# A decoder trunk in one core: the order of each stage's last sums, and where weights and memory are placed between stages

## The chip, the cores and the metric

The kernel runs on one core of a Trainium2 chip. The metric is the time of one execution in microseconds on the device; a time without further words is the median of several executions.

## The reference

Two layers work on 512 tokens of 1024 features, with 256 memory tokens beside them. Each layer is four steps, and each step ends in a layer normalization with a gain and a bias; `a` is the square root of 2.

```python
for i in range(DEPTH):                      # DEPTH = 2
    x = layer_norm(a * x + 0.5 * swiglu_ffn(x, ffn_w_in[i, 0], ffn_w_out[i, 0]), ...)
    h = diff_attention(x, ...) if i == 0 else pool_mixer(x, ...)
    x = layer_norm(a * x + h, ...)
    x = layer_norm(a * x + memory_cross_attention(x, mem, xa_wq[i], xa_wkv[i], xa_wo[i]), ...)
    x = layer_norm(a * x + 0.5 * swiglu_ffn(x, ffn_w_in[i, 1], ffn_w_out[i, 1]), ...)
```

`swiglu_ffn` is `(silu(x @ Wg) * (x @ Wu)) @ w_out` with 2816 hidden features. `diff_attention` (DA) has 8 heads with a rotary embedding and subtracts a second softmax from the first. `pool_mixer` takes causal means over 2, 4, 8 and 16 tokens and a small matrix for each group. `memory_cross_attention` has 4 heads, whose keys and values come from the memory. All is float32.

## The kernel before

**Numbers.** Every factor of a product is split in two parts of 32 bits with a shorter mantissa: `wh` or `xh`, a cast on ScalarE (L107), and `wl` or `xl`, the rest, a subtraction on VectorE (L108). A product is three matmuls (L163, L164, L165: high by high, low by high, high by low).

**Tiling.** The stream lies in four tiles `X` of 128 tokens by 1024 features. Weights come through DMA queues of SyncE (SP) and, where two blocks are added on the way, GpSimd (POOL), into raw tiles (`ra`, `rc`, `b`, `raw`), and are split into `wh` and `wl`. The FFN's matrices are multiplied by seven products of blocks in place of eight; lanes x, y and z are its products in work, and its factors of the stream (`factors`: `xh`, `xl`, `xe`) are sums and differences of blocks of X, made in `turn_factors` (L471 to L482). For that, X is transposed by TensorE (`pt<-ident,X`, L366), 128 by 128 at a time, eight for a token. `wh` of cross attention's keys and queries is made by L203 and L205.

**Stages.** There are eight: FFN, DA, cross attention, FFN; FFN, pool mixer, cross attention, FFN. Each stage ends with its *last sums*: for each token tile t and each half of the features, a matmul tile `ps` (18 matmuls of 512 columns in an FFN, 12 in attention) that VectorE adds to X (L312). After both halves of a token comes its LayerNorm, in `ln_token`: a mean (VectorE, L321), a Square with its sum (ScalarE, L328), two small GpSimd operations for the reciprocal root (L329, L330), and two scalings on VectorE, each in two instructions of 512 columns (L333, L336). Gain and bias are loaded in halves of 512 columns. For DA and cross attention as the next stage, the token is then transposed and split in `turn`. FFNs transpose and split all four tokens themselves at their start, with four ScalarE copies (L422) that keep raw blocks. In FFNs the sums are ordered by half and then by token; in the mixers' and attention's last half by token and then by half.

**Order.** Each engine has a queue, and works through it in order. The order in the queues is planned ahead by a scheduler, from the program's order, priorities and pools: a tile in a pool that takes over other tiles' place waits for their last readers. Cross attention's output weights (`raw<-in_xa_wo`, 4 x 512 rows) are split into tiles of the pool `w`, which FFN weights take over after it. `weave` runs a main sequence (keys and values of the memory, in layer 1) with a side sequence (pool mixer) between.

Of the kernel before, what the change touches and what calls it, by code (L numbers as in the profile page):

```python
# [44 lines left out]
GATES = {"xa": (1, 2)}  # L45

# [51 lines left out]
class Trunk:  # L98
# [33 lines left out]
    @contextmanager  # L132
    def stage_pools(self, raw, aux, w=5):

        pool = lambda name, **k: self.tc.tile_pool(name=name, bufs=1, reuse_waits="tile", **k)
        with pool("w") as self.wp, pool("raw") as self.rawp, pool("aux", space=PSUM) as self.auxp:
            self.w_bufs, self.raw_bufs, self.aux_bufs, self.aux_turn = w, raw, aux, 0
            yield
# [20 lines left out]
    def mm3(self, out, w, x, start, stop, again=False):  # L159
# [5 lines left out]
        mm(out, w[1], x[0], start=False, stop=stop, skip_group_check=again)  # L165
# [81 lines left out]
    def rows(self, w, k0, kn, c0):  # L247

        got = []
        for k in range(0, kn, 4):  # L250
# [29 lines left out]
    def load_row(self, tag, row):  # L280

        if tag in ("hr", "sr"):
            t = self.tmp(tag, (P, 2, S))
            got = [t[:, half] for half in range(2)]
        else:
            got = [self.tmp(tag) for _ in range(2)]
        for half, t in enumerate(got):
            src = row[None, half * S : (half + 1) * S]
            self.nc.sync.dma_start(t, src.to_broadcast([P, S]))
        return got  # L290

    def begin_ln(self, layer, i, scale):

        self.ln_scale = scale
# [10 lines left out]
        self.make_xt = not self.last_ln and self.ln_next in ("da", "xa")  # L305
# [10 lines left out]
    def ln_token(self, t):  # L316
# [5 lines left out]
        y = [X[:, half * S : (half + 1) * S] for half in range(2)]  # L322
# [8 lines left out]
        for half in range(2):  # L331
            c = slice(half * S, (half + 1) * S)
            nc.vector.scalar_tensor_tensor(y[half], X[:, c], mean, g[half], ALU.add, ALU.mult)  # L333
        for half in range(2):
            c = slice(half * S, (half + 1) * S)
            end = nc.vector.scalar_tensor_tensor(X[:, c], y[half], rstd, b[half], ALU.mult, ALU.add)  # L336
# [5 lines left out]
        if self.make_xt:  # L342
            self.late.append(t)

# [7 lines left out]
    def new_xt(self):  # L352
        self.xh = [self.xtp.tile([P, 4, S], F32R, tag="xh", name="xh") for _ in range(2)]
        self.xl = [self.xtp.tile([P, 4, S], F32R, tag="xl", name="xl") for _ in range(2)]

    def turn(self, t, half, two_pass=None):

        pt = self.aux("pt").rearrange("p (c n) -> p c n", c=4)
        c0 = half * S
        self.transpose4(pt, [self.X[t][:, c0 + j * P : c0 + (j + 1) * P] for j in range(4)])  # L360
        o = slice(t * P, (t + 1) * P)
        self.turned = self.split(self.xh[half][:, :, o], self.xl[half][:, :, o], pt)
# [6 lines left out]
    def to_tokens(self, parts, w, k0, kn, first, last, scale):  # L369

        nc = self.nc
        order = [(half, t) for half in range(2) for t in range(NT)]
        ws = [None, None]
        if last and kn == 4:
            order.sort(key=lambda x: x[1])
        for half, t in order:
            c, o = slice(half * S, (half + 1) * S), slice(t * P, (t + 1) * P)
            if t == 0:
                ws[half] = self.rows(w, k0, kn, half * S)
# [4 lines left out]
            if last:  # L384
                self.ln_add(t, half, scale if first else 1.0, ps)
                if half == 1:
                    if t < NT - 1:
                        self.turn_late()
                    self.ln_token(t)
# [7 lines left out]
    def ffn(self, layer, j, ln, beside=None):  # L397
        w_in, w_out = self.a["ffn_w_in"][layer, j], self.a["ffn_w_out"][layer, j]
        self.new_xt()
# [16 lines left out]
        for w in works + works[:1]:  # L416
            next(w)
        raw = [self.tmp("hb", (P, 4, 2 * P)) for _ in range(2)]
        pts = [self.turn_factors(t) for t in range(2)]
        for t in range(2):  # L420
            for half in range(2):
                self.nc.scalar.copy(raw[half][:, :, t * P : (t + 1) * P], pts[t][half])  # L422
# [20 lines left out]

    def factor_tiles(self):


        parts = []
        for x in (self.xh, self.xl):
            views = [t.rearrange("p a (b n) -> p (a b) n", n=2 * P) for t in x]
            got = [v[:, i : i + 4] for v in views for i in (0, 4)]  # L450
            parts.append(got + [self.act("xe", (P, 4, 2 * P)) for _ in range(3)])
        return list(zip(*parts))

    def turn_factors(self, t, raw=None):
# [5 lines left out]
        for half in range(2):  # L460
            tag = "px" if t in (0, 3) else ("py", "yz")[half]
            pt = self.aux("pt", tag).rearrange("p (c n) -> p c n", c=4)
            self.transpose4(pt, [self.X[t][:, half * S + j * P : half * S + (j + 1) * P] for j in range(4)])
            pts.append(pt)
        if t < 2:
            for half, pt in enumerate(pts):
                self.split(F[half][0][:, :, o], F[half][1][:, :, o], pt)
            return pts
# [16 lines left out]
    def up(self, w, u, lane, early):  # L485
# [19 lines left out]
        def operand(raw):  # L505
            v = self.hl([P, 4, H])
            self.split(v[0], v[1], raw)
# [13 lines left out]
        bank = lambda t: t.rearrange("p (j n) -> p j n", j=2)  # L521

# [6 lines left out]
        v = operand(ra)  # L529
        more(ra, 1, 2)  # L530
# [153 lines left out]
    def plain_down(self, w, layer, j, ln):  # L684
# [11 lines left out]
        for half in range(2):  # L696
# [14 lines left out]
            for t in range(NT):  # L711
                o = slice(t * P, (t + 1) * P)
# [624 lines left out]
```

## Time and profile before

| | us |
|---|---|
| median of 3 executions | 2026.42 (2024.79 to 2027.14) |
| the profiled execution | 2023.37 |
| its span, first to last instruction | 2021.6 |

| engine | busy share of the span |
|---|---|
| TensorE (PE), matmuls | 97% |
| TensorE, weight loads | 89% |
| VectorE (DVE) | 78% |
| ScalarE (ACT) | 51% |
| GpSimd (POOL) | 16% |

How to read the lines below: times run from the span's start. A timeline row has start, duration, engine, line of the kernel, operation, output<-inputs (without buffer numbers), partitions x elements, count, and in brackets the idle time ahead and what ended it. A row of waits has who waited for whom and the total, the number and the longest. PE's starts, not its durations, give its rate, since matmuls overlap.

### The profile page before, as it was taken

What the parts mean: (1) busy time and instruction counts of PE and PEld (TensorE: products, weight loads), DVE (VectorE), ACT (ScalarE), POOL (GpSimd) and SP (SyncE); (2) the same over time, 40 slices, a digit from 0 to 9 for tenths busy, and PEclk for the clock granted to TensorE, in tenths of its full rate; (3) what the DMA queues carried; (4) which work ended last, traced back from release to release, by engine and by line L of the source; (5) the groups of instructions that cost most, each with busy time, mean ns of one, the idle gap of its engine ahead of it and who ended that gap; (6) DMA issues with size and microseconds to landing.
All of it is one profiled execution on the core that took longest, in us unless ns stands there. A gap on an engine that the chain in (4) does not pass through costs nothing.

```text
span 2021.6 us, 32634 instructions
## 1 busy us (share of the span) xinstructions
PE 1961.3 (97%) x13104; PEld 1799.4 (89%) x13104; DVE 1570.6 (78%) x2260; ACT 1027.6 (51%) x1561; POOL 315.1 (16%) x305
## 2 busy tenths in 40 slices
PE   8999999999999998999999999999999999999997
PEld 8999998887878987999998899999799878999996
DVE  8988887888866548788887788888786566888885
ACT  6545454566645426554553555545454335555452
POOL 2111110122110002121121211111100013111211
PEclk9999999999999998999999999999989998999999
DMA  9877763222115335977774677876333319677861
GB/s 277 169 167 167 169 134 107 64 63 84 53 53 167 105 122 128 189 167 167 157 157 129 136 163 167 168 170 133 127 114 126 104 64 204 151 162 162 186 128 42
DMA packets 248455, 277.96 MB, mean 137 GB/s; under 512 B 8432, under 2 KB 212720, under 8 KB 248304
## 3 DMA queue, kind: packets, MB, share of 16 engines
q0 software_dynamic: 92928, 92.29, 29.7%
q1 hardware_dynamic: 155376, 183.59, 28.0%
q8 instruction: 103, 1.69, 0.3%
q14 instruction: 48, 0.39, 0.1%
HBM read 273.75 MB, written 2.10 MB: 136 GB/s over the span
## 4 chain that ended last, share of the span: by engine, by line
PE 67%; issue 19%; DVE 7%; ACT 4%; POOL 2%; DMA 1%; SPq 0%; POOLq 0%; DVEq 0%; ACTq 0%
PE x L165 8%; PE x L164 8%; PE x L163 8%; PE z L165 4%; PE z L164 4%; PE z L163 4%; PE px L163 3%; PE px L164 3%; PE px L165 3%; PE y L165 2%; PE ps L163 2%; PE y L163 2%; PE y L164 2%; PE ps L164 2%; PE ps L165 2%
## 5 line engine op out<-in xcount | busy, mean ns | idle before, releaser
L107 ACT CAST wh<-ra 128x1024 fp32r<-128x1024 f32 x184 | 193.1, 1049 | 235.3 <-PE x L164 70.1
L503 POOL DMA_DIRECT2D ra<-in_ffn_w_in_dram x132 | 170.1, 1312 | 839.3 <-DVE wl L108 797.4
L108 DVE TENSOR_TENSOR wl<-ra,wh 128x1024 fp32r<-128x1024 f32 x184 | 223.3, 1220 | 79.0 <-ACT wh L107 79.0
L107 ACT CAST wh<-rc 128x1024 fp32r<-128x1024 f32 x136 | 142.4, 1050 | 140.8 <-PE x L164 43.9
L163 PE MATMUL x<-xh,wh 128*128 128x256 f32 x704 | 202.3, 288 | 5.7 <-ACT wh L107 4.6
L165 PE MATMUL x<-xh,wl 128*128 128x256 f32 x704 | 202.3, 287 | 1.5 <-DVE wl L108 1.4
L164 PE MATMUL x<-xl,wh 128*128 128x256 f32 x704 | 201.9, 287 | 0.3 <-DVE xl L108 0.3
L165 PE MATMUL x<-xe,wl 128*128 128x256 f32 x704 | 199.2, 283 | 0.0
L164 PE MATMUL x<-xe,wh 128*128 128x256 f32 x704 | 199.2, 283 | 0.0
L163 PE MATMUL x<-xe,wh 128*128 128x256 f32 x704 | 199.1, 283 | 0.0
L107 ACT CAST wh<-b 128x1024 fp32r<-128x1024 f32 x112 | 117.5, 1049 | 153.2 <-PE x L164 77.8
L108 DVE TENSOR_TENSOR wl<-rc,wh 128x1024 fp32r<-128x1024 f32 x136 | 164.7, 1219 | 36.5 <-ACT wh L107 36.5
L108 DVE TENSOR_TENSOR wl<-b,wh 128x1024 fp32r<-128x1024 f32 x112 | 136.9, 1223 | 50.9 <-ACT wh L107 50.4
L108 DVE TENSOR_TENSOR wl<-raw,wh 128x1024 fp32r<-128x1024 f32 x76 | 95.3, 1263 | 69.5 <-ACT wh L107 68.8
L163 PEld LDWEIGHTS x<-xh,wh 128*128 128x128 f32 x704 | 137.8, 196 | 7.9 <-ACT wh L107 5.2
L165 PEld LDWEIGHTS x<-xh,wl 128*128 128x128 f32 x704 | 137.6, 196 | 2.6 <-DVE wl L108 2.6
L164 PEld LDWEIGHTS x<-xl,wh 128*128 128x128 f32 x704 | 137.7, 196 | 1.8 <-DVE xl L108 0.7
L164 PEld LDWEIGHTS x<-xe,wh 128*128 128x128 f32 x704 | 135.0, 192 | 1.3
L163 PEld LDWEIGHTS x<-xe,wh 128*128 128x128 f32 x704 | 135.0, 192 | 1.2
L165 PEld LDWEIGHTS x<-xe,wl 128*128 128x128 f32 x704 | 135.0, 192 | 0.0
L107 ACT CAST wh<-raw 128x1024 fp32r<-128x1024 f32 x76 | 79.2, 1049 | 92.0 <-PE xq L164 26.5
L329 POOL TENSOR_SCALAR var<-var 128x1 f32<-128x1 f32 x32 | 20.0, 626 | 584.4 <-ACT p L328 298.0
(372 smaller groups left out, 6237.2 us busy)
## 6 DMA issues: line engine op xcount, KB each, us to landing
ra<-in_ffn_w_in_dram POOLq DMA_DIRECT2D x132, 512.0 KB, 7.0
rc<-in_ffn_w_in_dram SPq DMA_DIRECT2D x88, 512.0 KB, 5.4
b<-in_ffn_w_out_dram SPq DMA_DIRECT2D x76, 512.0 KB, 4.4
ra<-in_ffn_w_in_dram SPq DMA_DIRECT2D x44, 512.0 KB, 3.7
rc<-in_ffn_w_in_dram POOLq DMA_DIRECT2D x44, 512.0 KB, 9.4
raw<-in_xa_wkv_dram SPq DMA_DIRECT2D x16, 1024.0 KB, 5.4
raw<-in_da_w_qkv_dram SPq DMA_DIRECT2D x16, 512.0 KB, 5.0
raw<-in_xa_wq_dram SPq DMA_DIRECT2D x8, 1024.0 KB, 4.8
```

Of the source, the lines that this page charges most:

```text
L107: self.nc.scalar.copy(hi, src),
L108: self.nc.vector.tensor_sub(lo, src, hi.bitcast(F32)),
L163: mm(out, w[0], x[0], start=start, stop=False, skip_group_check=again)
L164: mm(out, w[0], x[1], start=False, stop=False, skip_group_check=again)
L165: mm(out, w[1], x[0], start=False, stop=stop, skip_group_check=again)
L329: nc.gpsimd.tensor_scalar(var, var, 1.0 / D, EPS * self.ln_scale**2, ALU.mult, ALU.add)
L503: nc.gpsimd.dma_start(t, source(*block), accum_op=ALU.add)
```

## The change

1. The last sums of all stages come in one order, by (half, token): (0,0), (0,1), (1,0), (1,1), (0,2), (0,3), (1,2), (1,3). Token 0 is transposed just after the sum (0,3) was put in the queue and token 1 after (1,2).
2. FFNs take part in this: tokens 0 and 1 are transposed and split at the end of the stage before, and the FFN rebuilds their raw blocks by two additions xh + xl of 1024 columns on VectorE, in place of four ScalarE copies. These additions are placed behind the first weights' split.
3. Gain and bias are loaded as one tile of 1024 columns, and the scalings are one instruction each, save in the pool mixer and the last LayerNorm. Cross attention has a tag of its own for them (`gb`).
4. The last half of cross attention's output weights is split into tiles of the heads' tags (`q`, `kv`, `pT`), eight splits of 512 columns in place of four of 1024.
5. In layer 1 the order of the pools is raw, memory, weights; the memory is loaded first in the pool mixer at a high priority, and `weave` has other numbers (900 and 4300 for 1200).
6. Transposes and pool matmuls are placed behind the last matmul put out before them (`behind`); side pools wait by tile.

```diff
+LAST = ((0, 0), (0, 1), (1, 0), (1, 1), (0, 2), (0, 3), (1, 2), (1, 3))
+TURNS = ((0, 3), (1, 2))
...
-    def weave(self, main, side, gap):
+    def weave(self, main, side, gap, lead=0):
...
-        self.clock, credit, weight = 0, 0, 1.0
+        self.clock, credit, weight = 0, -lead, 1.0
...
+            if homes:
+                got += [home() for home in homes]
+                for j, t in enumerate(got):
+                    self.split(t[0], t[1], raw[:, j])
+                continue
...
-        self.make_xt = not self.last_ln and self.ln_next in ("da", "xa")
+        self.make_xt = not self.last_ln and self.ln_next != "pool"
...
+        if self.last_ln or not self.wide_gain:
+            cols = [slice(half * S, (half + 1) * S) for half in range(2)]
+        else:
+            cols = [slice(0, D)]
...
-        for half in range(2):
-            c = slice(half * S, (half + 1) * S)
-            nc.vector.scalar_tensor_tensor(y[half], X[:, c], mean, g[half], ALU.add, ALU.mult)
+        for i, c in enumerate(cols):
+            nc.vector.scalar_tensor_tensor(y[i], X[:, c], mean, g[i], ALU.add, ALU.mult)
...
+    def summed(self, half, t, scale, ps):
+
+        self.ln_add(t, half, scale, ps)
+        if self.late and (half, t) in TURNS:
+            self.turn_late(1 if (half, t) == TURNS[0] else 0)
+        if half:
+            self.ln_token(t)
...
+        with self.behind() if self.last_mm else nullcontext():
+            self.transpose4(pt, [self.X[t][:, c0 + j * P : c0 + (j + 1) * P] for j in range(4)])
...
-        order = [(half, t) for half in range(2) for t in range(NT)]
-        if last and kn == 4:
-            order.sort(key=lambda x: x[1])
-        for half, t in order:
+        for half, t in LAST if last else sorted(LAST):
...
+        self.turn_late(2)
+        self.late = []
+        next(works[0])
         raw = [self.tmp("hb", (P, 4, 2 * P)) for _ in range(2)]
-        pts = [self.turn_factors(t) for t in range(2)]
-        for t in range(2):
-            for half in range(2):
-                self.nc.scalar.copy(raw[half][:, :, t * P : (t + 1) * P], pts[t][half])
-        self.turn_factors(2, raw)
-        next(works[0])
-        self.turn_factors(3, raw)
+        act, dve = self.first_split
+        with self.tc.issue_after(act.ins), self.tc.issue_after(dve.ins):
+            for r, (hi, lo) in zip(raw, self.factors):
+                self.nc.vector.tensor_tensor(r, hi.bitcast(F32), lo.bitcast(F32), ALU.add)
+            self.turn_factors(2, raw)
         for w in works[1:]:
             next(w)
+        self.turn_factors(3, raw)
...
+        kv = lambda: tuple(self.kvp.tile([P, S], F32R, tag="kv", name="kv", bufs=8) for _ in range(2))
+        q, pT = (lambda: self.pair("q")), (lambda: self.pair("pT"))
+        homes = [[q] * 4, [kv, kv, kv, pT]]
...
-            self.later.enter_context(self.other_pools())
+            self.later.enter_context(self.other_pools(("raw", "mem", "w")))
...
                 side = self.pool_mixer(layer, ln)
+                with self.tc.high_priority():
+                    self.load_memory()
                 next(side)
-                self.load_memory()
                 self.kv = []
-                self.weave(self.early_kv(layer, 2), side, 1200)
+                self.weave(self.early_kv(layer, 2), side, 900, 4300)
```

More of the change, by code (lines that the diff above doesn't have):

```diff
@@ L384, in to_tokens @@
             if last:
[L385 to L389, printed above, removed]
+                self.summed(half, t, scale if first else 1.0, ps)
             else:
@@ L442, in ffn, with factor_views, turn_factors @@
         drain(works[0])
+    def factor_views(self):
+        views = [t.rearrange("p a (b n) -> p (a b) n", n=2 * P) for t in self.xh + self.xl]
+        got = [v[:, i : i + 4] for v in views for i in (0, 4)]
+        return list(zip(got[:4], got[4:]))
     def factor_tiles(self):
[L447 to L454, printed above, removed]
+        new = lambda: [self.act("xe", (P, 4, 2 * P)) for _ in range(3)]
+        return self.factor_views() + list(zip(new(), new()))
+    def turn_factors(self, t, raw):
         nc, F = self.nc, self.factors
@@ L506, in operand @@
             v = self.hl([P, 4, H])
-            self.split(v[0], v[1], raw)
+            splits.append(self.split(v[0], v[1], raw))
             return v
@@ L529, in up @@
         v = operand(ra)
+        if early and lane == 0:
+            self.first_split = splits[0]
         more(ra, 1, 2)
@@ L695, in plain_down, with operands @@
         self.begin_ln(layer, ln, 2.0)
-        for half in range(2):
+        def operands(half):
             ws = []
```

133 lines of the change are left out of this document (73 added, 60 removed).

## The prediction

> **What bounds the kernel now.** I read the page first, then the waits of TensorE stretch by stretch, the windows around the eight stage ends, and the timeline at four of them.
>
> ```profile
> span 2021.6 us, 32634 instructions
> PE 1961.3 (97%) x13104; PEld 1799.4 (89%) x13104; DVE 1570.6 (78%) x2260; ACT 1027.6 (51%) x1561; POOL 315.1 (16%) x305
> L107 ACT CAST wh<-ra 128x1024 fp32r<-128x1024 f32 x184 | 193.1, 1049 | 235.3 <-PE x L164 70.1
> out_dram<-X SPq DMA_DIRECT2D x8, 256.0 KB, 2.1
> ```
>
> TensorE is busy for 97% of the span and the change leaves its work alone, so only the holes can move, and they lie where one stage hands over to the next. The waits of TensorE there (total, times, longest), one fence for each hand-over: cross attention to second FFN in layer 0, first FFN to pool mixer, cross attention to second FFN in layer 1.
>
> ```profile
> PE pt L366 <- ACT hb L422: 4.6, 1, 4.6
> PE x L163 <- ACT wh L107: 2.3, 1, 2.3
> ```
> ```profile
> PE pp L1038 <- ACT xh L107: 2.8, 1, 2.8
> PE pp L1041 <- DVE xl L108: 2.7, 1, 2.7
> ...
> PE pt L1079 <- DVE X L312: 1.0, 1, 1.0
> ```
> ```profile
> PE z L163 <- DVE hr L545: 3.9, 1, 3.9
> ```
>
> Next, windows from the end of a stage's last sums (T0) to a milestone behind the hole: kernel start; first FFN to DA; DA to cross attention; into layer 0's second FFN; into layer 1's first FFN; pool mixer; into layer 1's second FFN. Columns: window, its length, busy time (count) by engine, granted clock, DMA share, GB/s.
>
> ```profile
> 0.00:42.20 42.20, 34.08 (x247) 32.68 (x248) 32.86 (x49) 29.06 (x42) 9.30 (x12) 0.96 1.06 292
> 340.00:360.00 20.00, 19.05 (x120) 16.04 (x119) 17.75 (x33) 8.38 (x15) 5.81 (x10) 1.00 0.19 60
> 604.80:622.10 17.30, 15.49 (x130) 14.79 (x128) 15.34 (x24) 10.76 (x16) 1.29 (x2) 1.00 0.56 182
> 771.40:811.70 40.30, 32.81 (x246) 31.36 (x244) 32.96 (x46) 28.82 (x42) 12.11 (x11) 0.87 0.74 171
> 1117.10:1153.70 36.60, 31.75 (x249) 30.64 (x248) 31.08 (x46) 24.89 (x40) 8.96 (x9) 0.95 0.49 119
> 1458.90:1480.00 21.10, 14.68 (x92) 13.63 (x90) 19.40 (x36) 12.69 (x21) 2.79 (x4) 0.76 0.59 185
> 1661.30:1703.80 42.50, 34.00 (x245) 32.70 (x243) 33.35 (x46) 28.31 (x42) 12.04 (x11) 0.88 0.97 229
> ```
>
> TensorE's rate, and the clock after a hole:
>
> ```profile
> 1116.93 0.39 PE L165 MATMUL ps<-ha,xe 128*128 128x512 f32 x1
> 1117.16 1.91 PE L366 MATMUL pt<-ident,X 128*128 128x128 f32 x16
> ...
> 1125.10 0.28 PE L163 MATMUL x<-xh,wh 128*128 128x256 f32 x1
> 1125.22 0.28 PE L164 MATMUL x<-xl,wh 128*128 128x256 f32 x1
> ```
> ```profile
> 776.80:787.10 10.30, 5.86 (x24) 5.16 (x25) 8.18 (x12) 7.75 (x13) 1.49 (x2) 0.50 0.05 6
> ```
> ```profile
> 1121.60:1125.00 3.40, 3.10 (x15) 2.70 (x14) 3.40 (x7) 2.69 (x5) 0.74 (x2) 0.50 0.02 5
> ```
> ```profile
> 1688.20:1691.60 3.40, 2.98 (x14) 2.68 (x14) 3.40 (x4) 0.62 (x1) 0.00 (x0) 0.50 0.87 302
> ```
>
> Starts differ by 0.23 us for a 512-column matmul and 0.12 for 256 columns; a transpose takes about 0.11. An FFN's opening (216 matmuls of 256 columns, 16 transposes) would thus take 27.7 us without holes; the windows show 36.6 to 42.5. After the 3.9 us wait the clock is 0.50 for 3.4 us: half of that, 1.7 us, is lost again. I charge 1.7 us behind every hole of 3 us or more.
>
> **The change part by part.** Prices for the chain that ends a stage, from the DA stage's end:
>
> ```profile
> 603.25 1.41 DVE L336 SCALAR_TENSOR_TENSOR X<-X,rstd,v 128x512 f32<-128x512 f32 x2 [0.44 <-POOL rstd L330]
> ...
> 605.91 0.21 DVE L321 TENSOR_SCALAR mean<-sums 128x1 f32<-128x1 f32 x1
> 606.05 1.22 DVE L205 TENSOR_TENSOR wl<-raw,wh 128x1024 fp32r<-128x1024 f32 x1
> 606.22 1.16 ACT L328 ACTIVATE rt<-X,mean 128x1024 bf16<-128x1024 f32 x1 [0.15 <-DVE mean L321]
> 607.18 0.68 DVE L108 TENSOR_TENSOR mem0l<-pt,mem0h 128x512 fp32r<-128x512 f32 x1
> 607.78 1.40 DVE L333 SCALAR_TENSOR_TENSOR X<-X,mean,v 128x512 f32<-128x512 f32 x2
> 607.85 0.58 ACT L107 CAST mem4h<-pt 128x512 fp32r<-128x512 f32 x1
> 609.10 1.41 DVE L336 SCALAR_TENSOR_TENSOR X<-X,rstd,v 128x512 f32<-128x512 f32 x2
> ```
>
> VectorE starts a 512-wide operation 0.60 us after the one before and a 1024-wide one 1.13 after; ScalarE takes 0.5 for a 512-wide cast, 1.05 for a weight cast. One LayerNorm takes mean 0.15, Square 1.35, the first scaling 1.3, GpSimd's two steps 1.7 beside it, the second scaling 1.3. One 1024-wide scaling in place of two 512-wide ones: I take 1.25 (floor 1.13, the weight subtract; ceiling 1.33), worth 0.1 a token.
>
> *The order of the last sums* puts tokens 2 and 3 side by side at the end. With sums of 4.1 us (FFN) or 2.7 us (attention, plus the two turned tokens in between), token 2's second scaling ends at T0+3.1 and token 3's add runs in the middle of it (T0+1.1 to 1.8); token 3's Square runs T0+3.4 to 4.75 and its second scaling ends at T0+7.9 to 9.0. Before, token 3's ended at T0+5.6 (610.5 against 604.85). What the planned order puts behind it on VectorE waits for that. The turns that are moved among the sums are hidden: token 1's LayerNorm ends at T0-4.5, its transposes come at T0-3.6, and no sum waits for its predecessor's buffer. Where in the old order sums waited for that, at both cross attention ends, the waits go; the row is layer 1's:
>
> ```profile
> PE ps L163 <- DVE X L312: 0.7, 2, 0.5
> ```
>
> With the smaller holes beside them (21.3 us before T0 whose matmuls need 19.9) I take 1.2 us at each.
>
> *DA to cross attention.* The low half of the first key weights (wl, 1.13) now stands behind token 3's second scaling: 8.1 to 9.25. Before it ran at T0+1.2. After the 16 memory transposes (1.75) TensorE can do only three matmuls until T0+9.25: 7.2 us empty. Then 93 matmuls (11.1), 16 transposes (1.74), and 1.7 for the clock: the first query matmul at T0+23.8 against 17.3. **6.5 us lost** (bounds 4.8 to 8).
>
> *Kernel start.*
>
> ```profile
> 11.04 1.09 PE L366 MATMUL pt<-ident,X 128*128 128x128 f32 x8 [0.83 <-DMA X<-in_x_dram]
> 16.42 0.59 ACT L539 COPY sp<-x 128x512 f32<-128x512 f32 x1 [1.29 <-PE x L165]
> ```
>
> The first product no longer waits for the third token's transposes, so it ends at 15.2, not 16.2. But the cast of the second lane's weights moves behind the copy of that product's result on ScalarE (15.4 to 17.0), its low half ends at 18.25, and the two additions that rebuild raw factors (2 x 1.13) replace four ScalarE copies on VectorE. Following VectorE's queue with 0.60 and 1.13 a step, the last lane's low half is done at 34.8 while TensorE has run dry at 30.9; 88 matmuls remain: 45.4, or 47.1 with the clock, against 42.2. I take 46.7: **4.5 lost** (2 to 5).
>
> *Cross attention to second FFN, layer 0.* Output weights in the heads' tiles: eight splits of 512 in place of four of 1024, 0.3 us more VectorE work, hidden under products. The first three loads no longer wait, yet the first cast is queued behind token 3's Square on ScalarE, its low half behind token 3's second scaling (7.9 to 9.05), and the third lane's cast behind the first product's copy. TensorE is empty until T0+9.1, runs dry again to 32.3, and reaches the milestone at 42.9 to 44.6, I take 43.8 against 40.3. With the 1.2 before T0: **2.3 lost** (0 to 3.5).
>
> *The same in layer 1.* There the casts stand before the LayerNorm, so products start at T0 at once and the hole moves: VectorE has, after token 3, the two additions and twenty operations of 0.6, and the last low half is done at T0+24, with TensorE dry from about 17.5. Milestone 34.5 to 36.7, I take 36.0 against 42.5, plus 1.2: **7.7 gained** (5 to 9). *Second FFN to layer 1's first* has the same queue and ends at 36.0 against 36.6: **0.6 gained** (-1 to 2).
>
> *First FFN to DA*: 119 matmuls need 17.5 of the window's 20 us; in the new order two tokens' factors are finished before T0 and only token 2's and 3's hold up the first v product, some 1.5 us instead of 2.5: **1.0 gained** (0 to 2).
>
> *Pool mixer, memory first.* The memory load waits for the weights of half 0, free at T0-8.2, and lands some 5 us later, so the 16 transposes go at T0. But the four memory splits on VectorE now stand before token 3's scalings, which end at 9.0, and the key weights' casts and splits behind its xh and xl: T0+11.2 and 12.65. TensorE is empty for 10.7 us where it now waits 1.0, 2.8 and 2.7 with half rate between. In the old window 88 matmuls after T0 need 9.1 of 20.8 us, so 11.7 are lost there and 1.6 more to 1490; in the new order 10.7 and 1.7: 12.4. **Nothing gained** (-3 to 3). At its end 0.7 of the 1.1 us wait of the first query product goes (0 to 1.5).
>
> *End of the kernel.*
>
> ```profile
> 2002.90 0.68 DVE L312 SCALAR_TENSOR_TENSOR X<-X,ps 128x512 f32<-128x512 f32 x1
> 2005.26 0.75 POOL L329 TENSOR_SCALAR var<-var 128x1 f32<-128x1 f32 x1 [3.73 <-ACT sp L328]
> 2006.09 0.94 POOL L330 TENSOR_TENSOR rstd<-var,mhalf 128x1 f32<-128x1 f32 x1
> ...
> 2008.40 0.68 DVE L312 SCALAR_TENSOR_TENSOR X<-X,ps 128x512 f32<-128x512 f32 x1
> 2009.19 0.39 PE L165 MATMUL ps<-ha,xe 128*128 128x512 f32 x1
> ```
>
> Each token's LayerNorm takes 5.5 us (2002.90 to 2008.40) but sums come every 4.1, so the four pile up and the span ends 12.4 us after the last matmul. In the new order tokens 0 and 1 are done early: token 2 begins 3.9 us before the last matmul ends, then 2 x 5.5 and 2.1 for the output's landing: 9.3. **3.1 gained** (2.5 to 3.5).
>
> Sum of gains, in the order of the parts: -6.5 -4.5 -2.3 +7.7 +0.6 +1.0 +0 +0.7 +3.1 = -0.2 us. The profiled execution took 2023.37 (span 2021.6 and 1.8 around it), 3.05 below the median 2026.42 of the three runs; the step is set against the median: 2026.6. About 0.2%, 4 us, is what a measurement of this kernel tells from no change.
>
> A page's rule on the clock: the Trainium skill, TensorE: Matmul & The Clock Gate, Part 1, says that the array falls to half rate after an idle window of about 3.4 us and needs about that long of sustained work to recover. The trace shows 0.50 after the 3.9 us wait, but also from 1121.6, after an idle time of only 2.3 us. By that rule the hole of 3.9 us at the kernel start is at the edge, and 46.7 there could be 45.4.
>
> **The rivals.** *Full clock in the late holes.* The holes at the kernel start and in three FFN openings are sprinkled with six or eight matmuls each; if these keep the clock up, 4 x 1.7 = 6.8 us of my charge is not paid: 2019.8. For it: DA's end ran with small waits (1.8 of its 17.3 us without a matmul) at 1.00; against it: the 3.9 us wait lost the clock.
>
> *Half rate lasts longer (slower).* From 776.8 to 787.1 the clock stays 0.50 for 10.3 us, since only 24 matmuls ran in it. The new holes at DA's end, in layer 0's second FFN, and in the pool mixer begin with two or three matmuls and then wait for low halves. If each holds half rate for one more stretch of 3.4 us, and so do the openings' second holes at the start and in layer 0, 5 x 1.7 = 8.5 us more: 2035.1. It decides once the matmuls after a hole come in broken groups.
>
> *The change does not do what it says in layer 1*: the tiles freed early don't bring the FFN's weights early, because the pool holding them opens only at T0; then the 7.7 us gain is gone: 2034.3. Against it: the loads' waits in the new order name matmuls of the half before.
>
> **How the numbers follow.** The sum 0.37 (its own range 2022 to 2032; 0.06 of it faster, 0.27 same, 0.04 slower), full clock 0.33 (0.30 faster, 0.03 same), longer half rate 0.20 (0.17 slower, 0.03 same), late weights 0.10 (0.08 slower, 0.02 same). Faster 0.36, same 0.35, slower 0.29. The range takes the fast rival with 5 us of the bounds and the slow one with 2: 2014 to 2037.
>
> **What would show it.** In the windows after: 23.8 us at DA's end, 44 into layer 0's second FFN, 36 into both of layer 1's, 9.3 behind the last matmul. Among the waits, `ACT hb` is gone, and a `DVE wl` wait of 5 us or more stands at DA's end. The prediction is wrong if DA's end costs under 2 us more, or if the layer 1 opening still takes 42.

## The result, and the profile after

The changed kernel takes 2035.3 us (median of 5 runs, 2034.06 to 2036.28); the kernel before, on the same chip, 2025.43 (2024.53 to 2027.14). The ratio is 1.0048 with a 95% interval of 1.0033 to 1.0062: slower by 10 us, where I had forecast 2026.6 and no change. The profiled execution took 2036.28, its span 12.9 us longer than the span before.

The page's head, of the changed kernel:

```profile
span 2034.5 us, 32534 instructions
...
PE 1966.0 (97%) x13104; PEld 1804.7 (89%) x13104; DVE 1575.2 (77%) x2228; ACT 1019.3 (50%) x1553; POOL 324.7 (16%) x305
```

TensorE has the same 13104 matmuls, so all of it lies in its holes and in the clock behind them. Windows of the changed kernel, from the last matmul of a stage's last sums (T0) to the matmul at which the window of before ended: kernel start, DA's end, into layer 0's second FFN, into layer 1's first, pool mixer, into layer 1's second FFN.

```profile
0.00:46.87 46.87, 36.74 (x247) 34.45 (x248) 34.75 (x51) 27.21 (x38) 9.46 (x12) 0.96 0.99 266
608.41:632.41 24.00, 18.06 (x131) 17.52 (x130) 18.63 (x24) 13.09 (x20) 2.12 (x4) 0.86 0.53 176
781.00:825.06 44.06, 33.50 (x235) 32.01 (x233) 34.34 (x42) 24.89 (x35) 13.64 (x12) 0.85 0.87 202
1132.48:1169.23 36.75, 31.49 (x234) 30.48 (x233) 29.49 (x38) 19.89 (x30) 10.39 (x9) 0.91 0.72 163
1474.89:1498.33 23.44, 13.56 (x91) 12.93 (x90) 20.27 (x28) 13.47 (x20) 2.23 (x4) 0.71 0.69 224
1681.27:1718.66 37.39, 31.76 (x234) 30.58 (x233) 30.05 (x38) 21.12 (x31) 10.95 (x9) 0.91 0.55 128
```

The lengths are nearly those that I wrote down: 46.9 (46.7 predicted), 24.0 (23.8), 44.1 (44), 36.8 and 37.4 (36 each). Only the pool mixer grew against its forecast. But look at the second column of counts, TensorE's matmuls: 235 and 234 in the FFN openings, against 246, 249 and 245 in the windows of before. The windows are as long as predicted and hold less work.

TensorE's waits of the changed kernel at DA's end, in layer 0's second FFN, in the pool mixer and in layer 1's second FFN:

```profile
PE pv L172 <- ACT wh L111: 4.6, 1, 4.6
PE pk L173 <- DVE mem0l L112: 1.3, 1, 1.3
```
```profile
PE x L172 <- ACT wh L111: 4.8, 1, 4.8
PE x L174 <- DVE wl L112: 2.7, 1, 2.7
```
```profile
PE pk L172 <- ACT wh L111: 9.4, 1, 9.4
PE pk L174 <- DVE wl L112: 0.5, 1, 0.5
```
```profile
PE z L172 <- DVE hr L578: 1.8, 1, 1.8
PE z L172 <- DVE xl L112: 1.5, 1, 1.5
PE y L174 <- DVE wl L112: 1.2, 1, 1.2
PE y L172 <- DVE xl L112: 1.0, 1, 1.0
```

Each of the first three is a stage's first weights, split late; the fourth is a row of small waits on VectorE where before there were 3.9 and 2.3. The `ACT hb` wait is gone, as predicted; the `DVE wl` wait of 5 us or more that I named for DA's end is not there.

To set one kernel against another without windows, I count TensorE's **time lost**: over neighbouring matmuls, the distance of their starts less the distance at full clock (0.2265 us for 512 columns, 0.1195 for 256, 0.108 for a transpose, and so on). Since the matmuls are the same 13104, the hand-overs can be cut at the same ordinal number in every trace, and work that is moved past T0 counts in neither. This loss holds the holes and what a lower clock costs. In us, for the two kernels and the experiments below (an end of a stage in the first column):

| | before | after | old_order | split_first | bands_free | old_opening | homes_only | homes_and_tail | losses_undone |
|---|---|---|---|---|---|---|---|---|---|
| kernel start | 8.1 | 12.9 | 11.2 | 13.1 | 14.1 | 7.7 | 9.3 | 7.2 | 9.2 |
| first FFN to DA | 2.9 | 2.1 | 2.5 | 2.1 | 2.0 | 2.1 | 2.9 | 2.9 | 2.2 |
| DA to cross attention | 7.4 | 13.6 | 8.2 | 10.4 | 14.0 | 12.1 | 7.5 | 6.2 | 8.2 |
| to layer 0's second FFN | 13.1 | 16.5 | 16.5 | 16.5 | 16.8 | 11.1 | 11.8 | 11.7 | 10.2 |
| to layer 1's first FFN | 7.5 | 9.2 | 8.2 | 9.2 | 9.2 | 7.5 | 9.7 | 9.4 | 6.4 |
| pool mixer | 13.5 | 17.6 | 17.5 | 17.6 | 12.5 | 17.6 | 13.2 | 13.0 | 13.7 |
| to layer 1's second FFN | 15.3 | 10.2 | 9.8 | 10.2 | 9.5 | 8.4 | 7.6 | 7.6 | 8.1 |
| all, to the last matmul | 88.2 | 103.4 | 93.7 | 100.3 | 99.3 | 87.9 | 81.9 | 78.5 | 79.0 |

Read with care: the start's opening is the same in after, split_first and bands_free and reads 12.9, 13.1 and 14.1; DA's end, the same in after, bands_free and old_opening, reads 13.6, 14.0 and 12.1. Differences under 2 us in one cell tell nothing by themselves. Each column is one profiled execution, which can lie some 3 us from the median of its kernel, as before's 2023.37 does. The time behind the last matmul fell from 12.4 to 10.2.

### The profile page after: what moved, and what is told of

The parts are those of the page before. It is cut to its first block, busy times and chain, and to the rows that moved or that the text cites. A ratio compares the mean times of both kernels' runs of the same rounds, so it can differ in the third digit from the quotient of the medians.

```text
span 2034.5 us, 32534 instructions
## 1 busy us (share of the span) xinstructions
PE 1966.0 (97%) x13104; PEld 1804.7 (89%) x13104; DVE 1575.2 (77%) x2228; ACT 1019.3 (50%) x1553; POOL 324.7 (16%) x305
## 5 line engine op out<-in xcount | busy, mean ns | idle before, releaser
L112 DVE TENSOR_TENSOR wl<-raw,wh 128x1024 fp32r<-128x1024 f32 x68 | 85.6, 1269 | 58.6 <-ACT wh L111 57.5
L350 POOL TENSOR_SCALAR var<-var 128x1 f32<-128x1 f32 x32 | 31.9, 996 | 507.5 <-ACT sp L349 248.9
L172 PE MATMUL z<-xh,wh 128*128 128x256 f32 x352 | 101.4, 288 | 10.8 <-DVE hr L578 4.8
```

The source lines that it names most:

```text
L112: self.nc.vector.tensor_sub(lo, src, hi.bitcast(F32)),
L172: mm(out, w[0], x[0], start=start, stop=False, skip_group_check=again)
L350: nc.gpsimd.tensor_scalar(var, var, 1.0 / D, EPS * self.ln_scale**2, ALU.mult, ALU.add)
```

## The experiments

My theory was that the loss comes from what stands on VectorE and ScalarE ahead of a stage's first weights, put there by the new order of sums and by the FFN's new opening; the rivals were that single parts (the order alone, memory first, the weights' tiles) do it. Each was timed in 5 rounds beside the kernel before; the ratios are to that.

**old_order**: the old order of the sums in the changed kernel.

```diff
-LAST = ((0, 0), (0, 1), (1, 0), (1, 1), (0, 2), (0, 3), (1, 2), (1, 3))
-TURNS = ((0, 3), (1, 2))
+LAST = tuple((half, t) for half in range(2) for t in range(4))
+TURNS = ((1, 1), (1, 2))
...
-        for half, t in LAST if last else sorted(LAST):
+        for half, t in sorted(LAST, key=lambda x: x[1]) if last else LAST:
```

> The changed kernel with the old order of the last sums and of the turns (FFN: half 0 of all tokens, then half 1; attention: token by token); homes, additions and memory first are kept. Theory A (the order puts the first weights' split behind token 3's LayerNorm): TensorE's hole at DA's end goes (6.5 us back), the first FFN's end loses 0.5, layer 0's second FFN gets 1 to 3 us back, the end of the kernel loses 2.2: about 2029 us against 2035.3. Rival B (the order is innocent, the new opening and the output weights' tiles cost the time): 2035 or above, since the gain at the kernel's end is given up.

Measured: 2032.29 us, 1.0035 (1.0023 to 1.0047). DA's end got its 5.4 us back, and the kernel's end gave up its gain. Layer 0's second FFN did not move (16.5): there the order is innocent. So A is right for DA and wrong for the FFN. As a whole, undoing the order gives back 3 of the 10 us.

**memory_late**: the pool mixer as before.

```diff
-            self.later.enter_context(self.other_pools(("raw", "mem", "w")))
+            self.later.enter_context(self.other_pools())
...
-                with self.tc.high_priority():
-                    self.load_memory()
                 next(side)
+                self.load_memory()
...
-                self.weave(self.early_kv(layer, 2), side, 900, 4300)
+                self.weave(self.early_kv(layer, 2), side, 1200)
```

> The changed kernel with the pool mixer's part undone: old order of the pools, memory loaded after the mixer's first step, the weave's gap of 1200 without a lead; all else kept. Theory A (memory first puts four memory splits ahead of token 3's scalings and the key weights' casts behind its xh): 2 us back in the pool mixer and up to 1.7 at its end: 2032 to 2033 us. Rival B (the prediction's: the new sum order alone sets the mixer's hole, memory first is worth nothing): 2035 us. Rival C (memory first is a gain that the new order's loss covers): 2037 or more.

Measured: 2034.46 us, 1.0050 (1.0037 to 1.0063). No change; the mixer still loses 18.5 us. So memory first is not the cause, as the prediction held. Rival B's other half, that the new order of the sums sets the mixer's hole, is not right either: with the old sums (old_order) it loses 17.5 too.

**homes_only**: the kernel before with cross attention's output weights in its heads' tiles (below, the homes), and the tag `gb` for gain and bias that goes with it.

```diff
+        kv = lambda: tuple(self.kvp.tile([P, S], F32R, tag="kv", name="kv", bufs=8) for _ in range(2))
+        q, pT = (lambda: self.pair("q")), (lambda: self.pair("pT"))
+        homes = [[q] * 4, [kv, kv, kv, pT]]
```

> The kernel before with one part alone: cross attention's output weights in the tiles of its heads (both layers), the LayerNorm's gain in a tile of its own. Theory A (layer 1's gain comes from the weights' tiles coming free early, so that the FFN's first casts stand before the LayerNorm): 5 to 8 us less in layer 1's opening, 0 to 2 less in layer 0's: 2018 to 2021 us. Rival B (the gain in layer 1 comes from the opening's two additions in place of four copies and from turns made earlier): within 1 us of 2025.4.

Measured: 2015.71 us, 0.9953 (0.9940 to 0.9965). TensorE's waits in layer 1's opening, and its window from T0 to the same matmul:

```profile
PE x L164 <- DVE xl L108: 1.5, 1, 1.5
PE y L165 <- DVE wl L108: 1.2, 1, 1.2
PE z L163 <- ACT wh L107: 1.0, 1, 1.0
```
```profile
1660.77:1697.44 36.67, 32.81 (x250) 31.34 (x249) 29.73 (x43) 24.83 (x39) 7.97 (x8) 0.95 0.53 126
```

ScalarE's first cast of the FFN's weights there, in the kernel before (T0 at 1661.3) and in homes_only (T0 at 1660.8):

```profile
1664.83 1.03 ACT L107 CAST wh<-ra 128x1024 fp32r<-128x1024 f32 x1
```
```profile
1639.60 2.00 ACT L107 CAST wh<-ra 128x1024 fp32r<-128x1024 f32 x2
```

The cast stood 3.5 us behind T0 and now stands 21 us ahead of it, as A says. The whole of layer 1's gain (15.3 to 7.6) comes with these tiles, with the old opening; the 1.3 of layer 0 is within the spread. The window does 250 matmuls in 36.7 us; the changed kernel's does 234 in 37.4.

**split_first**: the first key weights' cast and low half ahead of token 3's LayerNorm at DA's end.

```diff
-        with self.tc.issue_after(act.ins):
-            self.nc.scalar.copy(hi, src)
-        with self.tc.issue_after(dve.ins):
-            self.nc.vector.tensor_sub(lo, src, hi.bitcast(F32))
+        with self.tc.high_priority():
+            with self.tc.issue_after(act.ins):
+                self.nc.scalar.copy(hi, src)
+            with self.tc.issue_after(dve.ins):
+                self.nc.vector.tensor_sub(lo, src, hi.bitcast(F32))
```

> The changed kernel with one edit: the cast and low half of the first key weights of cross attention in layer 0 have priority, so that they stand on ScalarE and VectorE before token 3's mean and scalings at DA's end. Theory A (the hole there is VectorE's queue, the low half behind token 3's second scaling): the window at DA's end falls from about 24 to 18 us, some 6 us off the total: 2029 us. Rival B (the weights' DMA or the memory's transposes set it): no change, 2035. Rival C (the wait moves to token 3's LayerNorm, whose turns are due after the first key products): 1 to 3 us off, 2032 to 2034.

Measured: 2033.07 us, 1.0037 (1.0024 to 1.0049). Half of the expected: the hole there shrank by 3.2 us, and the wait took a new name. VectorE and TensorE's wait:

```profile
611.29 2.35 DVE L215 TENSOR_TENSOR wl<-raw,wh 128x1024 fp32r<-128x1024 f32 x2
613.56 0.20 DVE L337 TENSOR_SCALAR mean<-sums 128x1 f32<-128x1 f32 x1
613.68 0.68 DVE L112 TENSOR_TENSOR mem0l<-pt,mem0h 128x512 fp32r<-128x512 f32 x1
```
```profile
PE pk L173 <- DVE mem0l L112: 3.4, 1, 3.4
```

Priority moved both halves of the weights, 2.35 us, ahead of the memory's low half, for which the same products wait too. That is C's time, but the wait moved to the memory's low half and not to token 3's turns, as C had it. That VectorE's queue sets most of the hole is shown; this order of its operations moves the wait and doesn't end it.

**bands_free**: the fence of the pool mixer's band products taken out.

```diff
-            with self.behind():
+            with nullcontext():
                 for t in range(NT):
                     xh, xl = (x[:, o] for x in xs[half][t])
```

> The changed kernel without the fence that issues the pool mixer's band products behind the last matmul before them; all else kept (memory first, new order of sums). Theory A (the pool mixer's 4 us come from this fence: with it the key products, which wait for the weights' casts behind token 3, stand ahead of the band products on TensorE, and its hole of 9.4 us holds nothing; without it 36 band products of tokens 0 to 2 stand in it): 3 to 4 us back, 2031 to 2032 us. Rival B (VectorE's and ScalarE's queues set the time at which the key products can begin, and the band products are then still to be done elsewhere in the mixer's slack): no change, 2035. Rival C (the band products wait for token 3's factors and hold up the memory's key products): 2036 or more.

Measured: 2030.23 us, 1.0023 (1.0014 to 1.0032), and the mixer's loss fell from 17.6 to 12.5, against 13.5 before. The queue of TensorE in the changed kernel, with the fence:

```profile
1475.12 1.91 PE L1116 MATMUL pt<-ident,raw 128*128 128x128 f32 x16
1486.44 0.58 PE L172 MATMUL pk<-mem0h,wh 128*128 128x256 f32 x1 [9.41 <-ACT wh L111]
...
1495.88 0.23 PE L1074 MATMUL pp<-bandf,xh 128*128 128x144 f32 x1
```

Without it, the window, waits and the queue of TensorE:

```profile
1476.58:1494.60 18.02, 13.38 (x92) 12.69 (x91) 16.77 (x25) 10.84 (x17) 2.23 (x4) 0.81 0.59 194
```
```profile
PE pp L1074 <- ACT xh L111: 4.0, 1, 4.0
PE pp L1078 <- DVE xl L112: 0.4, 1, 0.4
```
```profile
1478.47 0.32 PE L1074 MATMUL pp<-bandf,xh 128*128 128x144 f32 x1
...
1486.66 1.13 PE L1074 MATMUL pp<-bandh,xh 128*128 128x128 f32 x4 [4.03 <-ACT xh L111]
...
1488.22 0.52 PE L172 MATMUL pk<-mem0h,wh 128*128 128x256 f32 x1
```

The 9.4 us hole now holds band products that don't need token 3, and a wait of 4.0 for token 3's factors. With the fence they stood behind the key products, whose weights are split last. That one line, which the description has in its point 6 and my prediction gave no term, costs 5 us, more than the mixer's whole loss of 4.1 (A).

**adds_on_gpsimd**: the opening's two additions moved off VectorE.

```diff
-                self.nc.vector.tensor_tensor(r, hi.bitcast(F32), lo.bitcast(F32), ALU.add)
+                self.nc.gpsimd.tensor_tensor(r, hi.bitcast(F32), lo.bitcast(F32), ALU.add)
```

> The changed kernel with the two additions that rebuild the raw factors in each of four FFN openings on GpSimd in place of VectorE. Theory A (the openings are bound by VectorE's queue, so 2 x 1.13 us taken from it come back at the kernel start and in layer 0's second FFN, and in part in layer 1): 3 to 7 us less, 2028 to 2032. Rival B (the openings wait for ScalarE's casts, which stand behind the first product's copy and behind token 3's Square, while VectorE idles): within 1.5 us of 2035. Rival C (GpSimd takes far longer than 1.13 us for 128x1024 and the third token's differences wait for it): 2037 or more.

Measured: 2040.80 us, 1.0073 (1.0060 to 1.0086), by C, and more than C: GpSimd holds VectorE up. Both engines in layer 0's opening:

```profile
790.20 5.62 POOL L454 TENSOR_TENSOR hb<-xh,xl 128x1024 f32<-128x1024 f32 x2
```
```profile
790.27 3.35 DVE L355 SCALAR_TENSOR_TENSOR X<-X,rstd,gb 128x1024 f32<-128x1024 f32 x1 [0.72 <-POOL rstd L351]
793.55 4.49 DVE L112 TENSOR_TENSOR wl<-ra,wh 128x1024 fp32r<-128x1024 f32 x2
```

An addition takes 2.8 us there, and VectorE's scaling 3.35 in place of 1.28. The openings of layer 1, where the additions fall beside less urgent work, lost 7.3 in place of 9.2 and 8.5 in place of 10.2. Each is within the spread, but both went the same way, so the 2.3 us taken from VectorE may count there. For the start and layer 0 the run decides nothing.

**second_cast_first**: at the start, the second lane's cast ahead of the first product's copy on ScalarE.

```diff
         p1 = sp()
-        nc.scalar.copy(p1, x)
+        with self.tc.issue_after(self.second_split[0].ins) if early and lane == 0 else nullcontext():
+            nc.scalar.copy(p1, x)
```

> The changed kernel with one order forced at each FFN's opening: the copy of the first lane's first product on ScalarE comes after the cast of the second lane's weights. It changes the order at the kernel start alone; the other openings have it already. Theory A (at the start ScalarE idles 5.5 us and VectorE 3.7 us because that cast stands behind the copy): the cast runs at 10 in place of 15.9 us, the low half at 13.3 in place of 17.0, and 1.5 to 3 us come back: 2032 to 2034 us. Rival B (the fence of the third token's transposes behind the first product holds VectorE's chain, so the cast's place costs nothing): within 1 us of 2035.

Measured: 2033.16 us, 1.0036 (1.0022 to 1.0051). The start lost 11.4; the unchanged start read 11.2 to 14.1 elsewhere. The time is A's, but inconclusive, and the edit did less than expected: the cast came at 13.60, not at 10, since the weights it casts had not landed.

```profile
13.60 1.05 ACT L111 CAST wh<-ra 128x1024 fp32r<-128x1024 f32 x1 [3.55 <-DMA ra<-in_ffn_w_in_dram]
```

**homes_and_tail**: homes_only, and the new order in the last stage alone.

```diff
+        for n, (half, t) in enumerate(LAST if self.last_ln else sorted(LAST)):
```

> The kernel before with two parts alone: cross attention's output weights in the tiles of its heads, and the new order of the sums in the last stage alone. Theory A (the parts are independent: homes gave 9, and in the last stage tokens 0 and 1 are normalized while tokens 2 and 3 are summed, which took 2.2 us off the end of the changed kernel): 2013 to 2014 us, with 10.2 us behind the last matmul. Rival B (the end was shortened by another part of the change): 2015.7 us as with homes alone, and 12.4 behind the last matmul.

Measured: 2013.03 us, 0.9934 (0.9921 to 0.9947); 9.6 us behind the last matmul (span 2008.8, last matmul at 1999.2). A: the end of the kernel is shorter by the order in the last stage, and the two parts add as far as the medians tell.

**old_opening**: the FFN's opening of the kernel before in the changed kernel.

```diff
-        self.turn_late(2)
-        self.late = []
-        next(works[0])
         raw = [self.tmp("hb", (P, 4, 2 * P)) for _ in range(2)]
-        act, dve = self.first_split
-        with self.tc.issue_after(act.ins), self.tc.issue_after(dve.ins):
-            for r, (hi, lo) in zip(raw, self.factors):
-                self.nc.vector.tensor_tensor(r, hi.bitcast(F32), lo.bitcast(F32), ALU.add)
-            self.turn_factors(2, raw)
+        pts = [self.turn_factors(t) for t in range(2)]
+        for t in range(2):
+            for half in range(2):
+                self.nc.scalar.copy(raw[half][:, :, t * P : (t + 1) * P], pts[t][half])
+        self.turn_factors(2, raw)
+        next(works[0])
...
```

> The changed kernel with the FFN's opening of the kernel before (tokens 0 and 1 turned inside the opening, four copies of raw factors on ScalarE in place of the two additions, transposes not fenced); order of sums, homes and memory first are kept. Theory A (the new opening costs at the start and in layer 0, and the homes alone gain in layer 1, by 7.7 as they did by themselves): start 4 to 5 us back, layer 0's second FFN 3 to 5, layer 1's second FFN 0 to 2.6: 2024 to 2027 us. Rival B (the prediction's: the new opening costs 4.5 at the start and about 2 in layer 0 but carries part of the gain of 7.7 in layer 1, so that its loss there is given back): 2029 to 2033. Rival C (the order of sums puts token 3's LayerNorm ahead of the first casts in every opening, old or new): 2033 or above.

Measured: 2021.58 us, 0.9980 (0.9970 to 0.9990): 13.7 us below the changed kernel, more than theory A gave, and now faster than before. The windows of the start and of layer 0's second FFN:

```profile
0.00:41.81 41.81, 33.91 (x248) 32.68 (x248) 32.90 (x49) 29.02 (x42) 9.35 (x12) 0.96 1.06 293
...
773.13:813.08 39.95, 34.52 (x250) 32.98 (x249) 34.23 (x44) 29.18 (x43) 12.65 (x13) 0.87 0.86 209
```

With 250 matmuls instead of 235, the opening of layer 0 is 4 us shorter. The new opening is the largest single loss: 5.2 us at the start, 5.4 in layer 0, and 1.7 and 1.8 in layer 1, within the spread. It gains nowhere that these runs can tell; B had still given it part of the gain in layer 1.

**losses_undone**: the changed kernel with the old opening, the band products free, and attention's sums token by token.

```diff
+        self.by_token = last and kn == 4
+        for half, t in sorted(LAST, key=lambda x: x[1]) if self.by_token else LAST if last else sorted(LAST):
...
```

The edits of old_opening and bands_free are in it too.

> The changed kernel with what the runs showed to cost time undone: the FFN's old opening, the old token-by-token order at the attention stages' ends, no fence on the band products; kept are the homes, memory first, the new order of sums at the FFN ends and wide scalings. Theory A (the losses add: opening 8 to 11, order at DA's end 5.5, fence 5): 2010 to 2014 us, level with homes and tail order alone (2013) or up to 3 below it, since the pool mixer's window without the fence lost 1 us less than before. Rival B (memory first and the FFN ends' new order cost about as much as they gain): 2013 to 2017 us.

Measured: 2011.96 us, 0.9932 (0.9919 to 0.9946), a time of A's, the lowest of all, though not told apart from homes_and_tail. Both are 13 to 14 us faster than before. What memory first, the wide scalings and the new order at the FFNs' ends add to that can't be measured here.

**opening_unfenced** and **unfenced_second_cast**: which part of the new opening is dear.

```diff
-            with self.behind():
+            with nullcontext():
                 self.transpose4(pt, [self.X[t][:, half * S + j * P : half * S + (j + 1) * P] for j in range(4)])
```

The second run has the edit of second_cast_first too.

> The changed kernel with one edit: in the FFN's opening the transposes of the third and fourth token are not fenced behind the last matmul before them; additions, early turns and all else stay. Theory A (the fence makes the new opening dear: the first product waits for a late low half, the transposes behind it start VectorE's chain of twenty operations only then; without it token 3's transposes fill the hole in layer 0 as in the old opening): 3 to 5 us back in layer 0's second FFN, 1 to 2 at the start: 2029 to 2031 us. Rival B (the additions on VectorE and the order of the casts make it dear): within 1 us of 2035.

> The edit of the opening without the fence together with the second lane's cast put ahead of the first product's copy. Theory A (fence and cast order are two causes at the start): the start loses 8 to 10 us in place of 12.9, layer 0's second FFN 12 to 14 in place of 16.5: 2027 to 2030 us. Rival B (the additions take VectorE's time in any order): the two edits together give no more than the 1.5 us of the cast alone, 2033.

Measured: 2034.61 (1.0039, 1.0027 to 1.0052) and 2033.70 (1.0034, 1.0023 to 1.0046). Without the fence layer 0's second FFN lost 14.3 in place of 16.5 in both runs; the start lost 14.3 and 13.5, so nothing came back there. By these two runs the fence is some 2.2 of layer 0's 5.4 us; by their times both are B's. The rest of the opening's loss goes with what these runs kept: the two tokens transposed before T0 and not in the hole (at most 1.7 us, an estimate from 16 transposes of 0.11), the two additions, and the order of casts around them. Which of these does how much stays open, since the run that moved the additions blocked VectorE. One candidate shows in layer 0's opening and was not tested there: ScalarE idles ahead of the copy of the first product, behind which the third lane's cast stands, for 7.0 us in the changed kernel and 2.2 in old_opening.

```profile
794.18 0.59 ACT L572 COPY sp<-x 128x512 f32<-128x512 f32 x1 [7.04 <-PE x L174]
```
```profile
789.56 0.59 ACT L574 COPY sp<-x 128x512 f32<-128x512 f32 x1 [2.21 <-PE x L174]
```

## Why the prediction was right in its windows and wrong in its sum

The time lay 8.7 us above the forecast, and slower was the outcome that I had given the least chance, 0.29. It lay in the range only by the slow rival's end of it: the sum's own range ended at 2032. That was luck, as the rival's mechanism cost less than half of its price (below). Between the two profiled executions 12.9 us were lost, where the sum had 0.2. By its steps (gain or loss predicted, and measured as time lost):

- **DA's end, -6.5: -6.2.** Right in mechanism and size. Token 3's second scaling and the low half behind it on VectorE, T0 being 608.41:

```profile
614.83 1.28 DVE L355 SCALAR_TENSOR_TENSOR X<-X,rstd,v 128x1024 f32<-128x1024 f32 x1
616.02 2.36 DVE L214 TENSOR_TENSOR wl<-raw,wh 128x1024 fp32r<-128x1024 f32 x2
```

The first low half ends some 8.8 us behind T0, predicted 9.25. The wait carries another name than I gave, `ACT wh`: a value product stands first in TensorE's queue, and its cast, whose load is late, ends at the same time:

```profile
615.90 2.00 ACT L111 CAST wh<-raw 128x1024 fp32r<-128x1024 f32 x2 [1.82 <-DMA raw<-in_xa_wkv_dram]
```
- **Kernel start, -4.5: -4.8.** Right in size, and old_opening shows that it is the opening. The steps came as written: the second lane's cast stands behind the copy at 15.92 (to 17.0), TensorE runs dry at 30.75 but for six matmuls (30.9 predicted) and goes on at 34.84 (34.8). What each of the opening's operations costs is open. Half rate came behind that hole, as I charged: the clock of the last row is 0.67.

```profile
15.92 1.05 ACT L111 CAST wh<-ra 128x1024 fp32r<-128x1024 f32 x1
```
```profile
34.84 0.39 PE L174 MATMUL y<-xh,wl 128*128 128x256 f32 x1 [0.63 <-DVE wl L112]
```
```profile
36.00:40.00 4.00, 4.00 (x25) 4.00 (x25) 2.58 (x6) 0.80 (x1) 1.28 (x1) 0.67 0.65 176
```

The 45.4 us that the Trainium skill's rule allowed (TensorE: Matmul & The Clock Gate, Part 1) did not come: the window is 46.87 us.

- **Layer 0's second FFN, -2.3: -3.4; layer 1's first, +0.6: -1.7; layer 1's second, +7.7: +5.1.** Here the step failed that compared windows. The new order transposes tokens 0 and 1 (16 transposes of 0.11 us, 1.7 us) before T0, which in layer 1's first opening is 1132.48:

```profile
1122.75 1.03 PE L403 MATMUL pt<-ident,X 128*128 128x128 f32 x8
...
1127.72 1.03 PE L403 MATMUL pt<-ident,X 128*128 128x128 f32 x8
```

I called these turns hidden because no sum waits for them. TensorE itself runs them, and TensorE is the bound: what leaves the window behind T0 is paid ahead of it. The count of an opening in the prediction, 216 products and 16 transposes, is that of the changed kernel; the windows of before hold 28 to 32 transposes. Windows of 36.8 and 36.6 us are not equal when one does 234 matmuls and the other 249. By the counts that is 1.2 to 1.6 us at each of three openings, some 4 us of the 12.7 (12.9 less 0.2) by which the sum missed. The 1.2 us of holes before T0 in cross attention did go (1.3 and 0.9). In layer 1 I also put the gain of the homes and the new opening into one number: by itself the first gave 7.7 and the second took 1.8 to 2.6.
- **Pool mixer, 0: -4.1.** The term was wrong; its own figures, 13.3 before and 12.4 after, even make a gain of 0.9. I followed VectorE's and ScalarE's queues, which came nearly as written (the first key product with a low half of the weights at T0+12.8, 12.65 predicted), and gave TensorE the same 88 matmuls in either order. The fence put the only ones that were ready behind the ones that were not, and I passed over the diff's line that does it: 5.1 us by bands_free. About 1.6 us are lost later, at two waits of the tokens' transposes (0.5 and 1.1) that before and memory_late don't have; in memory_late the part ahead of them loses more instead, 18.9 against 16.1 by the same count.
- **End of the kernel, +3.1: +2.2.** The mechanism is right: token 2's additions begin 3.7 us before the last matmul, at 2024.28, and token 3's 5.5 later:

```profile
2020.62 0.69 DVE L327 SCALAR_TENSOR_TENSOR X<-X,ps 128x512 f32<-128x512 f32 x1 [3.38 <-PE ps L174]
...
2026.15 0.68 DVE L327 SCALAR_TENSOR_TENSOR X<-X,ps 128x512 f32<-128x512 f32 x1
```

From there to the end it takes 8.3 us, not 5.5 + 2.1: the last token's path and its output were counted 0.7 short. The 12.4 us of before also run from the last matmul's start and the 3.9 to its end, 0.39 us later, so the sum gave 0.4 too much.
- **First FFN to DA, +1.0: +0.8. Pool mixer's end, +0.7: +0.3.** Right within what a profile tells. About 1 us more was lost in many small places.

The slow rival named nearly the time that came, 2035.1, but not by its mechanism. Intervals that are one and a half to 2.35 times the full-clock distance, taken for half rate, lose 21.8 us in all before and 25.7 after. That is 3.9 more, of which the sum had charged a part, where the rival asks for 8.5 beyond the sum. Half rate did last longer at DA's end: the clock was 0.50 from 617.0 to 622.2, 5.2 us in place of the 3.4 charged. The pool mixer, one of its five places, lost no more at half rate than before (2.6 against 2.8). Late weights were not the case: in layer 1's second FFN the first casts came at 1658.2, 23 us ahead of T0, and the gain is there. Full clock in the late holes was not the case either; the clock column of those four windows stands at 0.85 to 0.96, and the six matmuls in the start's hole did not keep it up.

## What to carry to other kernels

When the bound engine's own instructions are moved across the mark from which a window is measured, take their time out of the window, or count lost time between the same instructions in both kernels; hidden from waits isn't hidden from a busy engine. Price each part of a change alone: here one part was worth 9 us and another cost 14, and the whole showed 10. And look for a fence or an order that puts the work that is not ready ahead of the work that is: one such line cost 5 us here, in a hole of 9.4 us with nothing left to fill it.

## What the runs showed of the hardware

A GpSimd addition of 128x1024 took 2.8 us in adds_on_gpsimd, against 1.13 to 1.18 on VectorE, and VectorE's operations with two inputs in SBUF waited it out (3.35 in place of 1.28, 4.49 for two of 1.18). The Trainium skill, SBUF — State Buffer, SBUF: two separate sides, says that GpSimd and VectorE share a pair of ports under an exclusive lock, which a VectorE operation with two SBUF inputs needs against a GpSimd operation that reads SBUF. The trace agrees: both VectorE rows above start while an addition runs on GpSimd, and take 2.1 us longer each.

The clock after a hole is not the same from one profile to another. At layer 1's first opening homes_only has the instructions of before, and the same nearly empty 2.1 us; before, the clock stood at 0.50 for the 3.4 us behind it, and at 1.00 from 1125.0. In homes_only, three windows of 3.4 us from the same matmul on:

```profile
1120.90:1124.30 3.40, 2.15 (x15) 1.92 (x14) 3.40 (x7) 2.68 (x5) 0.74 (x2) 0.72 0.00 0
1124.30:1127.70 3.40, 3.40 (x18) 3.40 (x18) 2.26 (x5) 1.07 (x2) 0.00 (x0) 0.50 0.02 5
1127.70:1131.10 3.40, 3.40 (x25) 3.40 (x25) 2.69 (x4) 2.50 (x5) 0.00 (x0) 0.77 0.00 0
```

The half rate comes later and meets full work, and by the count of long intervals above the opening loses 2.9 us to it in place of 1.2. A charge for the clock behind one hole is uncertain by that much.
